# Moving the tiles of a fused decoder layer within the 128-byte grid of on-chip memory

## The chip, the cores and the metric

The kernel runs on one core of one Trainium2 chip. A core has a matrix engine (TensorE, "PE" in the profile; its weight loads are shown apart as "PEld"), three engines for element-wise work (VectorE "DVE", ScalarE "ACT", GpSimd "POOL"), and queues that move data between the chip's main memory and the on-chip memory, which has 128 partitions. The metric is device microseconds of one execution, as the median of the runs.

## The reference

One decoder layer on 256 tokens of 2048 channels, in float32:

```python
hn = rmsnorm(h, attn_norm_w)
u, c_q, c_kv, k_pe = split(hn @ w_in)              # 2048 -> 1024 + 512 + 256 + 64
y_ssm = s5_group(u, ...)                           # 64 groups, diagonal complex scan, GELU, gated unit
y_mla = mla_group(c_q, c_kv, k_pe, ...)            # 8 heads, latent queries, keys, values, causal
h = h + concat(rmsnorm(y_ssm), rmsnorm(y_mla)) @ w_out
a = causal_conv3(rmsnorm(h) @ w_up) + conv_b       # 2048 -> 2 x 5632
gate, val = split(a)
h = h + (silu(gate) * val) @ w_down                # 5632 -> 2048
out = rmsnorm(h, final_norm_w)
```

## The kernel before

Nearly all the work is products with about 180 MB of float32 weights, each read once. The weights come in *chunks* of 128 partitions x 1024 values (512 KB), in a fixed order (`w_in`, the latents' weights, `w_out`, `w_glu`, `w_up`, `w_down`). SP loads a chunk into a tile `raw`. L150 (ACT) rounds it to a part `hi` in a shorter format, L151 (DVE) makes the rest `lo = raw - hi`. Activations are split in the same way. A product is then the sum of three: hi x hi, hi x lo and lo x hi, which `mm3` issues at L165, L166 and L168. So a chunk costs 24 products of 128x128 with 128x256.

`PE.matmul(out, loaded, streamed)` becomes two instructions: a weight load (LDWEIGHTS) that puts the first operand into the array, and a MATMUL that streams the second one past it. In this text *loaded* and *streamed* mean these two operands. Which tile takes which part changes on the way:

- **Input, latents, output projection, gated unit, up-projection** (`mm3`, L165 to L168): `hi` and `lo` of the weights are loaded, 256 tokens of activations are streamed (`xh`/`xl`, `chl`, `ym`, `yhl`, `ys`, `x2h`/`x2l`).
- **Values** (`v_chunk`, L855 to L857): the activations `chl` are loaded, 512 columns of the weights are streamed.
- **Down-projection** (`down`, L1122): the gate's output `hid` (two tiles, `hid0` and `hid1`, the parts hi and lo) is loaded, 512 columns of the weights are streamed. There are four groups of 22 chunks and 12 products per chunk. In the last group the second half of the tokens uses products of 256 columns, and 10 of its 22 chunks have their `hi` and `lo` in tiles `xw` instead (`extra`).

The other parts (state space, attention) run as steps between the chunks up to about 270 us; the string `STEPS` says how many follow each chunk. In the up-projection each of 44 rounds takes four chunks, and its 96 products are followed by the convolution and the gate on ACT, DVE and POOL (`abuf`, `cv`, `hid`; L1069 to L1085).

Tiles are allocated from pools, which are stacked in a partition in the order in which they are opened: `const` (small tables, with the packed parameters `pk` first), `wp` (`hi`, `lo`, `raw`), `mid` (`uT`, `u4`, `yT`), `cpool` (`cA`, `scr`, `chl`, `qpt`), `sp` (the state space's tiles, later `ys`). After `left1.close()` the place from `mid` on is used again by `fp` (`abuf`, `cv`), `hp_` (`hid`) and `wx` (two more `raw` buffers: two of each five chunks from then on use them). `r0` (`xh`, `xl`, `x2h`, `x2l`, `ym`, `yhl`, `hT`, `ho`, `xw`) is stacked from the other end. A tile's place is rounded up to a multiple of 32 bytes. So a tile that grows moves every tile that is stacked after it.

Of the kernel before, what the change touches and what calls it, by code (L numbers as in the profile page):

```python
# [11 lines left out]
F32 = mybir.dt.float32  # L12
# [5 lines left out]
PSUM = bass.MemoryType.PSUM  # L18

P = 128  # L20
# How many steps of the state space follow each chunk of weights until its output is needed: the chunks
# of u, of the latents, of keys, values and queries, the last heads, the attention half of the output.
# [15 lines left out]
# Column layout of the packed per-partition parameters.  # L38
# [16 lines left out]
def layer_kernel(ctx: ExitStack, tc: tile.TileContext, pack, pos, xt, bk, w_in, w_kpe, w_uqn,  # L55
# [17 lines left out]
    # every chunk: 128 partitions x up to 1024 values, split exactly into two float32r parts  # L73
# [53 lines left out]
    def load_after(dst, src):  # L127
        """A load that stays behind the weights asked for so far."""
        with tc.issue_after(state["last"]):
            SP.dma_start(dst, src)  # L130

    def w_prep_to(n):
        while state["prep"] < min(n, len(chunks)):
            i = state["prep"]
            w_dma_to(i + 1)
            raw = raws.pop(i)
            if i == KPE_AT + 1:
                # the rotary key is a float32 product with the input rows as they are: its weights take the norm's
                wt = wp.tile([P, 1024], F32, tag="hi", name="wt")
                V.tensor_tensor(out=wt.rearrange("p (k n) -> p k n", n=64),  # L140
                                in0=raw.rearrange("p (k n) -> p k n", n=64),
                                in1=prm("attn_w").unsqueeze(2).to_broadcast([P, 16, 64]), op=ALU.mult)
                splits[i] = (wt, None)
            else:
                if i >= last_down and (i - last_down) % 6 >= 3:
                    hi, lo = extra[(i - last_down) % 6 - 3]
                else:
                    hi = wp.tile([P, 1024], F32R, tag="hi", name="hi")
                    lo = wp.tile([P, 1024], F32R, tag="lo", name="lo")
                A.copy(hi, raw)  # L150
                V.tensor_tensor(out=lo, in0=raw, in1=hi.bitcast(F32), op=ALU.subtract)  # L151
                splits[i] = (hi, lo)
            state["prep"] += 1
            w_dma_to(i + 1 + (5 if more else 3))
# [7 lines left out]
    def mm3(ps, wh, wl, xh, xl, nk, first, last):  # L162
        """ps += sum over k of w[k].T @ x[k], each operand given as two parts."""
        for k in range(nk):
            PE.matmul(ps, wh(k), xh(k), start=(first and k == 0), stop=False)  # L165
            PE.matmul(ps, wh(k), xl(k), start=False, stop=False)  # L166
        for k in range(nk):
            PE.matmul(ps, wl(k), xh(k), start=False, stop=(last and k == nk - 1))  # L168
# [5 lines left out]
    pk = const.tile([P, NPACK], F32, name="pk")  # L174
# [6 lines left out]
    def quads(dtype, name):  # L181
        """Sixteen row tiles, four to a tile."""
        ts = [r0.tile([P, 4, T], dtype, tag=f"xh{i}", name=f"{name}{i}") for i in range(4)]
        return lambda k: ts[k // 4][:, k % 4, :]
# [10 lines left out]

    cA = cpool.tile([P, 2048], F32, tag="cA", name="cA")
    A.dma_start(pk[:, 0:NA0], pack[:, 0:NA0])
    # the first half of the input rows and of three column tiles arrive two row tiles at a time
# [27 lines left out]
    # a few products of ones bring the array to its full clock before the data is there  # L226
# [19 lines left out]
    def tok_sums(parts, ps=None):  # L246
        """Sums over partitions and parts, token t of the half h in column h of a PSUM tile."""
        ps = wk_bank() if ps is None else ps
        for h in range(2):
            for i, a in enumerate(parts):  # L250
                PE.matmul(ps[:, h:h + 1], a[:, 128 * h:128 * h + 128], ones[:, 0:1], start=(i == 0),
                          stop=(i == len(parts) - 1))
        return ps[:, 0:2]

    def tok_rsqrt(ps, n, eps=None):
        """1 / sqrt(ps / n + eps) by token."""
        r = const.tile([P, 2], F32, tag="rtok", bufs=6, name="rtok")
        A.activation(r, ps, AF.Sqrt, bias=eps_t if eps is None else eps, scale=1.0 / n)
        V.reciprocal(out=r, in_=r)
        return r  # L260

    def tok_rows(r):
        """The values by token as a row, alike in every partition."""
# [6 lines left out]
    def row_scale(dst, parts, n, eps=None):  # L270
        """dst[p, t] = 1 / sqrt(sum over partitions and parts / n + eps), alike in every row."""
# [4 lines left out]
    def split_scaled(hi, lo, src, w):  # L276
        """hi + lo = src * w (one value of w per partition), hi in float32r."""
# [26 lines left out]
    def wrap(dst, src, k):  # L304
        """dst = src less the nearest multiple of 2 pi."""
# [14 lines left out]
    # factors of the complex products, the second set for the imaginary part of the other operand  # L320
# [6 lines left out]
    def ssm_setup():  # L327
# [21 lines left out]
        # columns: powers 0..4 of the state layout, then the key layout, each step with its own power  # L349
# [9 lines left out]
        # phase of a chunk of four steps in turns, and in two parts of which one has few bits  # L359
# [24 lines left out]
        # z = (abar - 1) / lambda  # L384
# [18 lines left out]
        # z times the powers, pair index outermost: [re | -im] and [-im | -re]  # L403
# [23 lines left out]
    # cos and sin of i * phi for the 64 chunks, eight pairs at a time  # L427
# [28 lines left out]
    # matrices of the state space, four pairs of groups at a time  # L456
# [8 lines left out]
    def ssm_in_products(b):  # L465
        """Chunk inputs to states times abar, laid [(step, p32), ...]: the two halves of the complex products."""
# [18 lines left out]
    def ssm_out_mats(b, c):  # L485
        """States (times abar) to outputs: C z abar^l, real (c = 0) and negated imaginary part."""
# [40 lines left out]
    def ssm_k(b):  # L527
        """Lag matrices: values of input b against C z abar^l."""
# [11 lines left out]
    def ssm_m(b):  # L540
        """Within a chunk: lag matrices placed by step, the skip on the diagonal."""
# [70 lines left out]
    def ssm_main():  # L612
        """Three steps per batch, each meant to follow one chunk of weights."""
# [54 lines left out]
    def u_pre(i):  # L668
# [8 lines left out]
        elif i == 8:  # L677
            load_after(pk[:, NA1:], pack[:, NA1:])
# [35 lines left out]
    def kpe_chunk():  # L714
        """The 64 channels of the rotary key, twice: even row tiles on one half of the array's columns, odd on the other."""
# [56 lines left out]
    # The latents stay without their scales by token: that of the queries goes into the softmax, those  # L772
    # of keys and values are applied where these leave PSUM.
# [9 lines left out]
    def c_norm():  # L783
        """rx / sqrt(mean((rx * latent) ** 2) + eps) by token, of the queries and of keys and values."""
# [11 lines left out]
        # of the two halves of the tokens the second comes first, as in the scores  # L796
# [33 lines left out]
    # queries and keys of two heads to a tile; their outputs, scaled and in two parts, take their place  # L830
# [170 lines left out]
    # sigmoid(z) = (1 + tanh(z / 2)) / 2; the group is held doubled until its norm  # L1001
# [47 lines left out]
    abuf = [fp.tile([P, 2, T + 2], F32, name=f"abuf{i}", bufs=1) for i in range(2)]  # L1049
# [38 lines left out]
    # Tokens on the partitions, two halves of them; the channels as (a, row tile, i), where 32 a + i is the  # L1088
    # partition a channel had. One group of weights has the 512 channels of one a.
# [4 lines left out]
    def ho_load():  # L1094
        """The residual to tokens on partitions: blocks of 32 x 32 turned, then moved."""
# [18 lines left out]
    # sums of squares: three groups and the two halves of the last  # L1114
# [19 lines left out]
    def finish(h, m):  # L1134
        """The norm by token: m of the sums ahead of the last."""
# [16 lines left out]
    # in the last group the second half of the tokens stays behind, and has a bank for each half of the channels  # L1152
# [120 lines left out]
```

## Time and profile before

| | |
|---|---|
| median of 3 runs | 1112.39 us (1111.87 to 1112.79) |
| span of the profiled execution, first to last instruction | 1111.5 us |
| instructions, TensorE products among them | 20545, 8264 |
| TensorE busy | 1066.4 us, 96% of the span |
| VectorE, ScalarE, GpSimd busy | 736.2, 611.0, 286.0 us |
| moved by DMA | 195.40 MB, mean 176 GB/s |
| mean granted TensorE clock | 0.991 of full speed |

The profiled execution is told by its span alone; what lies around the span shows only in that the runs' median is 0.9 us longer. A MATMUL row's duration covers the whole way of a product through the array, and the next product starts long before it ends. The *pitch*, from the start of one product to the start of the next, is what a product costs in a row of them. The timeline merges neighbours that are alike into one row with a count, so the pitch is the difference of two rows' starts by the count. The row of stages below (windows) gives each engine's busy time in a stretch with the number of its instructions.

### The profile page before, as it was taken

Reading aid. Unit: us, or ns where it says so; the run is one execution under the profiler, and the core shown is the slowest. Engines: PE = TensorE matmul, PEld = TensorE weight load, DVE = VectorE, ACT = ScalarE, POOL = GpSimd, SP = SyncE. Lnnn points to the kernel's source line nnn. Section 1 sums busy time; section 2 is a strip of 40 time slices with the busy share of each in tenths; the row PEclk is TensorE's granted clock in tenths of the full one; section 3 lists DMA queues with packets and bytes.
Section 4 is the critical chain, followed back from the end, with each engine's and each line's share of the span. In section 5 each row is a group of like instructions: output and inputs, shape, how many; then the busy total and the mean of one; then the engine's idle time right before and its main releaser. Section 6 shows DMA issues by size and latency. Waiting matters only on the chain.

```text
span 1111.5 us, 20545 instructions
## 1 busy us (share of the span) xinstructions
PE 1066.4 (96%) x8264; PEld 1002.9 (90%) x8264; DVE 736.2 (66%) x998; ACT 611.0 (55%) x986; POOL 286.0 (26%) x284
## 2 busy tenths in 40 slices
PE   7979899787999999999999999999999999999997
PEld 7979877786999999999999999999999888888896
DVE  8999898797798665656566565665657545454543
ACT  6567578857765645555555455555554434343433
POOL 7371745773333121211212112121211000000000
PEclk9989999999999999999999999999999999999999
DMA  6635341433555455555555555555555965555652
GB/s 211 227 115 172 134 130 61 171 134 131 173 176 186 172 189 189 174 188 180 182 189 183 180 189 174 188 189 180 182 182 185 258 227 189 189 189 189 210 190 76
DMA packets 56672, 195.40 MB, mean 176 GB/s; under 512 B 6528, under 2 KB 8448, under 8 KB 56576
## 3 DMA queue, kind: packets, MB, share of 16 engines
q1 hardware_dynamic: 54576, 190.93, 50.0%
q10 hardware_dynamic: 2000, 3.16, 1.1%
q8 instruction: 65, 1.06, 0.4%
q14 instruction: 31, 0.25, 0.1%
HBM read 189.86 MB, written 2.10 MB: 173 GB/s over the span
## 4 chain that ended last, share of the span: by engine, by line
PE 78%; DVE 11%; ACT 5%; issue 3%; DMA 3%; POOL 0%; SPq 0%; ACTq 0%; DVEq 0%
PE mm L168 18%; PE mm L166 18%; PE mm L165 18%; PE mm L1122 11%; PE wk L1122 11%; DVE lo L151 3%; ACT yT L610 1%; DMA bkt<-in_bk_dram 1%; DVE epad L477 1%; PE wk L913 1%; DVE hT L992 1%; PE wk L912 1%; ACT u L512 1%; DMA raw<-in_w_in_dram 1%; DVE sh L578 1%
## 5 line engine op out<-in xcount | busy, mean ns | idle before, releaser
L151 DVE TENSOR_TENSOR lo<-raw,hi 128x1024 fp32r<-128x1024 f32 x329 | 411.4, 1252 | 256.0 <-ACT hi L150 253.5
L150 ACT CAST hi<-raw 128x1024 fp32r<-128x1024 f32 x329 | 343.4, 1047 | 305.8 <-PE mm L166 113.2
L166 PE MATMUL mm<-x2l,hi 128*128 128x256 f32 x1408 | 345.6, 283 | 0.0
L165 PE MATMUL mm<-x2h,hi 128*128 128x256 f32 x1408 | 345.6, 283 | 0.0
L165 PEld LDWEIGHTS mm<-x2h,hi 128*128 128x128 f32 x1408 | 270.3, 192 | 0.0
L166 PEld LDWEIGHTS mm<-x2l,hi 128*128 128x128 f32 x1408 | 270.3, 192 | 0.0
L168 PE MATMUL mm<-x2h,lo 128*128 128x256 f32 x1408 | 197.6, 283 | 0.0
L168 PEld LDWEIGHTS mm<-x2h,lo 128*128 128x128 f32 x1408 | 181.6, 192 | 0.0
L1083 POOL TENSOR_TENSOR cv<-cv 128x256 f32<-128x256 f32 x44 | 68.0, 1545 | 389.4 <-ACT cv L1082 375.8
L1122 PE MATMUL wk<-hi,hid 128*128 128x512 f32 (+1 forms) x360 | 88.1, 364 | 0.0
L1122 PE MATMUL mm<-hi,hid 128*128 128x512 f32 x312 | 85.4, 395 | 0.0
L1122 PEld LDWEIGHTS wk<-hi,hid 128*128 128x128 f32 x360 | 63.5, 188 | 13.0
L1069 DVE TENSOR_TENSOR abuf<-mm,r 128x512 f32<-128x512 f32 x43 | 29.7, 691 | 62.2 <-PE mm L168 62.2
L1122 PEld LDWEIGHTS mm<-hi,hid 128*128 128x128 f32 x312 | 57.8, 188 | 13.1
L1075 ACT ACTIVATE cv<-abuf,pk 128x256 f32<-128x256 f32 x88 | 48.3, 595 | 28.5 <-DVE abuf L1069 26.9
L1084 ACT CAST hid<-cv 128x256 fp32r<-128x256 f32 x44 | 17.9, 406 | 75.1 <-POOL cv L1083 71.8
L1122 PE MATMUL wk<-lo,hid 128*128 128x512 f32 (+1 forms) x180 | 50.9, 364 | 0.0
L165 PE MATMUL mm<-xh,hi 128*128 128x256 f32 x184 | 48.0, 294 | 2.5 <-ACT hi L150 2.5
L1122 PE MATMUL mm<-lo,hid 128*128 128x512 f32 x156 | 49.0, 395 | 0.0
L166 PE MATMUL mm<-xl,hi 128*128 128x256 f32 x184 | 47.6, 292 | 0.0
L493 POOL TENSOR_TENSOR m<-bkt,pp 128x256 f32<-128x256 f32 x32 | 30.2, 955 | 61.2 <-DMA bkt<-in_bk_dram 47.2
L610 ACT ACTIVATE yT<-wk 32x64 f32<-32x64 f32 x128 | 35.6, 278 | 7.8 <-PE wk L604 6.3
(330 smaller groups left out, 1641.4 us busy)
## 6 DMA issues: line engine op xcount, KB each, us to landing
raw<-in_w_up_dram SPq DMA_DIRECT2D x176, 512.0 KB, 3.2
raw<-in_w_down_dram SPq DMA_DIRECT2D x88, 512.0 KB, 4.2
raw<-in_w_out_dram SPq DMA_DIRECT2D x32, 512.0 KB, 3.3
raw<-in_w_in_dram SPq DMA_DIRECT2D x25, 512.0 KB, 3.3
bkt<-in_bk_dram SPq DMA_DIRECT2D x8, 512.0 KB, 5.6
raw<-in_w_glu_dram SPq DMA_DIRECT2D x8, 512.0 KB, 3.3
raw<-in_w_uqn_dram SPq DMA_DIRECT2D x4, 512.0 KB, 4.3
hT<-in_xt_dram SPq DMA_DIRECT2D x4, 512.0 KB, 4.9
```

What stands on the lines that cost most here:

```text
L150: A.copy(hi, raw)
L151: V.tensor_tensor(out=lo, in0=raw, in1=hi.bitcast(F32), op=ALU.subtract)
L165: PE.matmul(ps, wh(k), xh(k), start=(first and k == 0), stop=False)
L166: PE.matmul(ps, wh(k), xl(k), start=False, stop=False)
L168: PE.matmul(ps, wl(k), xh(k), start=False, stop=(last and k == nk - 1))
L493: G_.tensor_tensor(out=m, in0=ci[:, s].unsqueeze(2).to_broadcast([P, 4, 4, 16]), in1=pp[:, s, c].rearrange("p (q l) -> p q l", l=4)[:, cb, ...
L610: A.activation(dst[:, j], psy[32 * j:32 * j + 32, q], AF.Gelu_apprx_tanh)
L1069: V.tensor_tensor(out=a[:, :, 2:T + 2], in0=ps, in1=r2.unsqueeze(1).to_broadcast([P, 2, T]), op=ALU.mult)
L1075: A.activation(t, a[:, gv, 2:T + 2], AF.Identity, bias=prm("conv_b", ch_, 1), scale=prm("conv_w", 176 + ch_, 1))
L1083: G_.tensor_tensor(out=cv[0], in0=cv[0], in1=cv[1], op=ALU.mult)
L1084: A.copy(hid[0][:, i, :], cv[0])
L1122: PE.matmul(ps[:, 0:n], hid[x][:, 2 * i + k, ts_], w[wk][:, 512 * k + c0:512 * k + c0 + n], start=(i == 0 and s == 0 and k == 0), stop=(i ...
```

## The change

Three tiles grow by bytes that nothing reads, and so what is stacked after them moves. The engines' instructions, their order, their sizes and their waits are those of before; only places differ, and with them the step from partition to partition of two tiles.

```diff
-    pk = const.tile([P, NPACK], F32, name="pk")
+    pk = const.tile([P, NPACK + 16], F32, name="pk")
...
+    cpool.tile([P, 16], F32, name="gap")
     cA = cpool.tile([P, 2048], F32, tag="cA", name="cA")
...
-            load_after(pk[:, NA1:], pack[:, NA1:])
+            load_after(pk[:, NA1:NPACK], pack[:, NA1:])
...
-    abuf = [fp.tile([P, 2, T + 2], F32, name=f"abuf{i}", bufs=1) for i in range(2)]
+    abuf = [fp.tile([P, 2, T + (12, 2)[i]], F32, name=f"abuf{i}", bufs=1) for i in range(2)]
```

The rest of the diff takes out comments; the line numbers in this text up to the next section are those of the kernel before. `pk` grows by 64 bytes per partition, `gap` takes another 64, `abuf0` grows by 80 (64 after rounding). The places that the two built programs give, in bytes from a partition's start, with the remainder by 128 and by 512:

| tiles | first byte before | mod 128, mod 512 | first byte after | mod 128, mod 512 |
|---|---|---|---|---|
| `hi`, `lo` of `wp` (first `hi`) | 30432 | 96, 224 | 30496 | 32, 288 |
| `raw` of `wp` (first) | 55008 | 96, 224 | 55072 | 32, 288 |
| `raw` of `wx` (first) | 169760 | 32, 288 | 169888 | 32, 416 |
| `uT`, `u4`, `yT` of `mid` (`uT`) | 67296 | 96, 224 | 67360 | 32, 288 |
| `chl` | 91872 | 96, 224 | 92000 | 96, 352 |
| `ys` | 108256 | 96, 224 | 108384 | 96, 352 |
| state space's tiles of `sp` (`epad`) | 108256 | 96, 224 | 108384 | 96, 352 |
| `xh`/`x2l`/`ym`/`qk` of `r0` (first) | 180192 | 96, 480 | 180192 | 96, 480 |
| `xl`/`hT`/`xw` of `r0` | 196576 | 96, 480 | 196576 | 96, 480 |
| `x2h`/`yhl`/`ho` of `r0` | 212960 | 96, 480 | 212960 | 96, 480 |
| `hid0` | 79648 | 32, 288 | 79776 | 32, 416 |
| `hid1` | 124704 | 32, 288 | 124832 | 32, 416 |
| `abuf0`, `abuf1` | 67296, 69376 | 96 and 0 (mod 128) | 67360, 69504 | 32 and 0 (mod 128) |
| `kpe` of `const` | 26912 | 32, 288 | 26976 | 96, 352 |

Slices of these tiles start a multiple of 512 bytes further on (128 columns) or of 1024 (256 columns), so all slices that a product takes have their tile's remainder by 512.

## The prediction

> **What bounds the kernel now.** I read the page's first sections, then one table of the stages, then the timeline of TensorE inside the long stages, and last the chain of waits in the short ones.
>
> ```profile
> PE 1066.4 (96%) x8264; PEld 1002.9 (90%) x8264; DVE 736.2 (66%) x998; ACT 611.0 (55%) x986; POOL 286.0 (26%) x284
> ...
> PEclk9989999999999999999999999999999999999999
> ...
> PE 78%; DVE 11%; ACT 5%; issue 3%; DMA 3%; POOL 0%; SPq 0%; ACTq 0%; DVEq 0%
> ```
>
> TensorE is busy nearly throughout, it is 78% of the chain that ends last, and its clock is granted at 90% or more in nearly every slice. The stages (input, latents and heads, attention half of the output with the state space, gated unit, state-space half of the output, up, down, the last group of down):
>
> ```profile
> core 0: us, PE busy (x) PEld busy (x) DVE busy (x) ACT busy (x) POOL busy (x), PEclk, DMA share, GB/s
> 0.00:116.80 116.80, 103.07 (x800) 97.99 (x801) 104.81 (x164) 78.25 (x131) 62.14 (x73) 0.96 0.52 177
> 116.80:174.00 57.20, 51.89 (x439) 43.62 (x438) 51.75 (x89) 40.47 (x86) 34.31 (x34) 1.00 0.37 123
> 174.00:269.00 95.00, 79.61 (x977) 72.14 (x978) 76.75 (x126) 69.52 (x200) 60.93 (x64) 0.98 0.33 116
> 269.00:303.50 34.50, 31.49 (x244) 30.72 (x243) 26.35 (x36) 26.84 (x55) 8.56 (x10) 0.95 0.58 201
> 303.50:350.40 46.90, 46.90 (x394) 46.90 (x393) 44.10 (x66) 28.69 (x48) 16.61 (x15) 1.00 0.52 179
> 350.40:858.00 507.60, 507.60 (x4233) 507.60 (x4232) 310.95 (x402) 265.96 (x356) 101.98 (x88) 1.00 0.53 183
> 858.00:1043.80 185.80, 185.80 (x799) 149.76 (x799) 92.36 (x87) 77.15 (x84) 1.48 (x2) 1.00 0.64 204
> 1043.80:1103.60 59.80, 59.80 (x394) 54.07 (x392) 27.21 (x29) 21.71 (x27) 0.00 (x0) 1.00 0.42 148
> ```
>
> From 303.5 us on TensorE never idles. The up-projection alone is 507.6 us, with VectorE busy 61% and ScalarE 52%: there a product's pitch is the time. The change can act only through that pitch, so the question is whether the pitch depends on the places of the two operands. The program before already holds products with different places. In the timeline of TensorE, the up-projection (loaded `hi`/`lo` at 96, streamed `x2h`/`x2l` at 96):
>
> ```profile
> 500.09 1.12 PE L168 MATMUL mm<-x2h,lo 128*128 128x256 f32 x8
> 501.05 0.28 PE L165 MATMUL mm<-x2h,hi 128*128 128x256 f32 x1
> ```
>
> Eight products in 0.96 us: a pitch of 120.0 ns, for 256 columns. In the last group of down (loaded `hid` at 32, streamed `xw` or `hi`/`lo` at 96):
>
> ```profile
> 1062.37 1.53 PE L1122 MATMUL wk<-xw,hid 128*128 128x256 f32 x12
> 1063.73 1.56 PE L1122 MATMUL mm<-xw,hid 128*128 128x512 f32 x6
> 1065.13 0.62 PE L1122 MATMUL wk<-hi,hid 128*128 128x256 f32 x4
> 1065.59 0.39 PE L1122 MATMUL wk<-lo,hid 128*128 128x256 f32 x2
> 1065.81 0.62 PE L1122 MATMUL wk<-hi,hid 128*128 128x256 f32 x4
> ```
>
> Twelve products of 256 columns in 1.36 us are 113.3 ns each, and six with `hi` and `lo` in 0.68 us are 113.3 again. Same shape, same type, one weight load per product: 6.67 ns less. It makes no difference whether the streamed tile lies at byte 196576 or 30432; the remainder by 128 is what these rows have in common and the up-projection has not. The weight loads agree:
>
> ```profile
> L165 PEld LDWEIGHTS mm<-x2h,hi 128*128 128x128 f32 x1408 | 270.3, 192 | 0.0
> ...
> L1122 PEld LDWEIGHTS wk<-hi,hid 128*128 128x128 f32 x360 | 63.5, 188 | 13.0
> ```
>
> 192 ns where both operands stand at 96, 188 ns where they stand 64 apart.
>
> For 512 streamed columns it is the other way round. The six products at 1063.73 us above (loaded 32, streamed 96) take 1.40 us, 233.3 ns each. The values stream 512 columns with both operands at 96:
>
> ```profile
> 155.07 0.40 PE L855 MATMUL mm<-hi,chl 128*128 128x512 f32 x1
> ...
> 156.46 0.39 PE L855 MATMUL mm<-hi,chl 128*128 128x512 f32 x1
> ...
> 169.50 0.39 PE L857 MATMUL mm<-lo,chl 128*128 128x512 f32 x1
> ...
> 170.86 0.39 PE L857 MATMUL mm<-lo,chl 128*128 128x512 f32 x1
> ```
>
> The first six, from 155.07 to 156.46 us, have 231.7 ns; the last six, from 169.50 to 170.86 us, 226.7 ns. Twice the pitch of 113.3 is 226.7, so these run free and the down-projection pays 6.67 ns per product, again. Why the sign turns is not shown; the table allows one reading: with 256 columns the loads run without a break (PEld 507.60 of 507.60 us), so each load trails its product, while with 512 they pause (149.76 of 185.80) and each starts along with its product.
>
> **The change part by part.** No instruction is added, removed or reordered on any engine or queue; every term is a count times a pitch.
>
> *Up.* `hi`/`lo` go to 32, `x2h`/`x2l` stay at 96. By 512 that is 288 loaded and 480 streamed, exactly the pair of `hid` and `xw` above. 44 x 4 x 24 = 4224 products x 6.67 ns = **28.2 us**; TensorE has no idle time there, so all of it shows if the chunks keep up. Who waits for whom in 356 to 866 us, then in 866 to 1109 us:
>
> ```profile
> ACT hi L150 <- PE mm L166: 82.6, 47, 1.9
> ...
> ACT hi L150 <- PE wk L1122: 109.7, 63, 3.5
> ...
> ACT xw L150 <- DMA raw<-in_w_down_dram: 5.6, 3, 2.8
> ```
>
> ScalarE waits for TensorE to free a buffer, not TensorE for ScalarE. The stage would take 479.4 us and need 183 x 507.6 / 479.4 = 194 GB/s; down already moves 204.
>
> *Down, 512 columns.* Streamed `hi`/`lo` come to 32, where `hid` stays: equal places, as in the values. The first three groups have 66 x 12 = 792 products x 6.67 ns = 5.3 us gained. In the last group 12 chunks have their parts in `wp`: 72 more such products gain 0.5 us, and 144 products of 256 columns go to equal places and lose 1.0 us. The 10 `xw` chunks keep their places. Together **4.8 us** gained. Bounds: the row of 226.7 ns on one side; on the other, equal places cost 512 columns another 6.67 ns, which is 864 x 6.67 = 5.8 us and the 1.0 us lost. I take the values' row, since it is the only one with 512 columns and equal places, and six products after a change of pattern were still at 231.7.
>
> *The stages before.* All other streamed activations (`xh`, `xl`, `chl`, `ym`, `yhl`, `ys`) end at 96 over weights at 32 and can gain only where products carry the chain. The chain of waits in 116.8 to 174, 174 to 269, 269 to 303.5 and 303.5 to 350.4 us:
>
> ```profile
> by line: PE wk L912 10.1%; PE wk L913 10.0%; DMA bkt<-in_bk_dram 8.9%; PE mm L168 7.1%; DVE lo L151 7.0%; PE mm L166 6.9%; PE mm L165 6.8%; issue 6.1%; DVE gm L481 3.7%; POOL m L493 3.3%; PE mm L855 3.2%; PE mm L856 3.2%; PE mm L857 3.2%; D
> ...
> by line: issue 15.7%; ACT yT L610 12.7%; DVE hT L992 8.0%; DVE lo L151 7.2%; DVE epad L477 6.0%; DVE sh L578 4.5%; ACT mt L552 4.3%; DVE scr L991 3.8%; DVE e L471 3.6%; PE wk L913 2.6%; DVE ta L569 2.5%; DVE tb L570 2.5%; DVE gm L481 2.5%;
> ...
> by line: PE mm L168 30.7%; PE mm L166 23.1%; PE mm L165 20.8%; ACT yT L610 12.9%; ACT hi L150 5.5%; ACT yhl L1009 4.8%; DVE yhl L1010 2.0%; issue 0.8%
> ...
> by line: PE mm L168 33.0%; PE mm L166 33.0%; PE mm L165 32.7%; PE wk L266 0.9%; PE wk L251 0.7%
> ```
>
> Products are 74.6% of 34.5 us in the gated unit: 25.7 us, 214 products, **1.4 us**. In the state-space half of the output they are all of it, 384 products, 2.6 us; but VectorE is busy 44.1 of 46.9 us and would have 44.3 left, so it is late next: I take half, **1.3 us**. In the heads 20.8% of 57.2 us is 99 products, 0.7 us, less 24 value products that lose up to 6.67 ns: **0.5 us**. Between 174 and 269 us and before 116.8 us products hardly carry the chain: **0.2 us**, and at most another 3 us if waits close up.
>
> *Other engines.* Whether a place costs them is seen at L151, which reads `raw` at 96 for three of five chunks and at 32 for two. Five in a row in the up-projection:
>
> ```profile
> 501.86 1.22 DVE L151 TENSOR_TENSOR lo<-raw,hi 128x1024 fp32r<-128x1024 f32 x1
> ...
> 504.57 1.22 DVE L151 TENSOR_TENSOR lo<-raw,hi 128x1024 fp32r<-128x1024 f32 x1
> ...
> 507.81 1.23 DVE L151 TENSOR_TENSOR lo<-raw,hi 128x1024 fp32r<-128x1024 f32 x1 [2.02 <-ACT hi L150]
> ...
> 510.05 1.23 DVE L151 TENSOR_TENSOR lo<-raw,hi 128x1024 fp32r<-128x1024 f32 x1 [1.02 <-ACT hi L150]
> ...
> 513.38 1.22 DVE L151 TENSOR_TENSOR lo<-raw,hi 128x1024 fp32r<-128x1024 f32 x1
> ```
>
> 1.22 or 1.23 us in all: nothing is put down for them.
>
> The sum is 28.2 + 4.8 + 1.4 + 1.3 + 0.5 + 0.2 = 36.4 us. The span of 1111.5 becomes 1075.1; with the 0.9 us by which the median of the runs is longer, **1076.0 us**.
>
> **The rivals.** *A, as above.* Chance 0.68, 1071 to 1080 us.
>
> *B, up gains but down does not.* After the change the operands of down agree by 128 but not by 512 (288 and 416), while those of the values agreed by both. Without the 4.8 us the time is 1080.8; at the far bound (6.8 us lost instead) 1087.6. Chance 0.14.
>
> *C, nothing happens.* The 6.67 ns might come from something else that sets the two stages apart, such as 24 products in a row into one bank of results against 6. Against it: the values, six in a row into one bank, have both 231.7 and 226.7. Time 1112.4, chance 0.05. The Trainium skill has a rule that speaks for this rival ("TensorE: Matmul & The Clock Gate", section "Step-by-step: what each phase is for"): the array reads the streamed operand and the weights by two independent ports, and loading the next weights does not take bandwidth from the running product. By that rule no place could matter and the sum would be zero; the rows of 113.3 and 120.0 ns, alike in all but the tiles, do not fit it.
>
> *D, slower.* One mechanism: equal places cost 6.67 ns at any width, and up's 120.0 ns has another cause. Then down pays 5.8 + 1.0 us and the time is 1119. It decides once up gains less than 6.8 / 4224 = 1.6 ns per product. For it speaks that equal places are what up has now; against it the 226.7 of the values. Chance 0.04.
>
> *E, the chunks come late.* Up's gain turns into waits of L150 for `raw`; with half of it left, 1090 us. Against it the 204 GB/s of down. Chance 0.06.
>
> **How the numbers follow.** The remaining 0.03 lies below 1071, if the early stages close up by more. The range 1071 to 1088 holds A and B, 0.82. A, B, E and the rest are faster by over 0.2% (2.2 us, about what a measurement of this kernel can tell from no change): 0.91. C is within it, 0.05, and D beyond, 0.04.
>
> **What would show it.** Right: rows of eight L168 products 0.91 us apart, weight loads of 188 ns in up, the stage 28 us shorter; six products of 512 columns in 1.36 us; products of 256 columns with `hi` in the last group at 120. Wrong: 120.0 ns in up (C, D), 233 or 240 in down (B), or idle TensorE with L150 waiting for DMA (E).

## The result, and the profile after

| | before | after |
|---|---|---|
| median (range) | 1112.33 us (1111.87 to 1112.79, 4 runs) | 1101.42 us (1100.62 to 1102.56, 4 runs) |
| span of the profiled execution | 1111.5 us | 1098.8 us |
| mean granted TensorE clock | 0.991 | 0.983 |

The time ratio is 0.9896 (0.9882 to 0.9910): about 11 us faster, where 36.4 us had been predicted. The sign is right, the size is not, and the time lies above the range. The two spans in the table differ by 12.7 us, more than the medians, because the profiled execution of after is the fastest of its four. The page of the kernel after, in the lines that answer to those shown of before (busy time by engine, then shares of the chain that ended last):

```profile
PE 1056.1 (96%) x8264; PEld 993.3 (90%) x8264; DVE 736.6 (67%) x998; ACT 611.5 (56%) x986; POOL 285.1 (26%) x284
...
PE 80%; DVE 9%; ACT 5%; DMA 3%; issue 2%; POOL 0%; SPq 0%; ACTq 0%; DVEq 0%
```

The counts are those of before; TensorE is busy for 10.3 us less and VectorE, ScalarE and GpSimd for the same time within 1 us. The windows by stage (input, latents and heads, attention half with the state space, gated unit, state-space half, up, three groups of down, last group):

```profile
core 0: us, PE busy (x) PEld busy (x) DVE busy (x) ACT busy (x) POOL busy (x), PEclk, DMA share, GB/s
0.00:116.60 116.60, 102.67 (x799) 97.47 (x800) 104.66 (x164) 78.57 (x131) 62.55 (x74) 0.93 0.53 177
116.60:174.20 57.60, 53.40 (x441) 44.92 (x439) 52.81 (x89) 40.77 (x88) 33.16 (x34) 0.97 0.37 123
174.20:269.50 95.30, 81.10 (x976) 73.97 (x976) 77.01 (x126) 69.36 (x200) 60.83 (x64) 0.93 0.35 115
269.50:301.10 31.60, 28.55 (x243) 27.73 (x242) 25.91 (x36) 26.60 (x55) 8.53 (x10) 1.00 0.65 218
301.10:347.20 46.10, 46.10 (x395) 46.10 (x394) 44.19 (x66) 28.78 (x48) 16.64 (x15) 1.00 0.55 183
347.20:845.00 497.80, 497.80 (x4233) 497.80 (x4232) 310.85 (x402) 266.09 (x356) 101.96 (x88) 1.00 0.56 187
845.00:1030.40 185.40, 185.39 (x800) 150.04 (x799) 92.99 (x88) 77.55 (x84) 1.48 (x2) 1.00 0.65 207
1030.40:1091.20 60.80, 60.80 (x393) 55.21 (x391) 26.23 (x29) 21.69 (x28) 0.00 (x0) 1.00 0.42 141
```

Up is 9.8 us shorter instead of 28.2. Down as a whole is 0.6 us longer instead of 4.8 shorter (0.4 gained, 1.0 lost). The gated unit is 2.9 us shorter, the state-space half 0.8. TensorE still has no idle time in up, so what is missing there is pitch and no wait. These are windows of one execution each: the shorter gated unit stands at a granted clock of 1.00 beside 0.95 before, which is taken up below. The timeline of TensorE at the start of up says more:

```profile
346.25 1.10 PE L168 MATMUL mm<-ys,lo 128*128 128x256 f32 x8
...
349.02 1.07 PE L168 MATMUL mm<-x2h,lo 128*128 128x256 f32 x8
...
351.74 1.07 PE L168 MATMUL mm<-x2h,lo 128*128 128x256 f32 x8
...
354.46 1.07 PE L168 MATMUL mm<-x2h,lo 128*128 128x256 f32 x8
...
357.18 1.07 PE L168 MATMUL mm<-x2h,lo 128*128 128x256 f32 x8
358.09 0.50 PE L254 MATMUL wk<-ones,hacc 128*128 128x1 f32 x4
...
360.41 1.11 PE L168 MATMUL mm<-x2h,lo 128*128 128x256 f32 x8
```

The starts of 349.02, 351.74, 354.46 and 357.18 us are 2.72 us apart, and 24 products lie in each step: 113.3 ns, the predicted pitch. Then four float32 products of one column pass (`wk<-ones,hacc`, the row sums of a norm). From there to the end of up, but for a gap in the second round where more products of the norm pass, the starts are 117 to 119 ns apart and the mean pitch is 117.8 ns, with the same tiles at the same places. One weight load in three then takes 192 ns and the others 187 or 188, so that the mean of up falls between the two values that the prediction named:

```profile
L165 PEld LDWEIGHTS mm<-x2h,hi 128*128 128x128 f32 x1408 | 266.5, 189 | 0.0
```

The timeline in the first groups of down, and in the last group (each kernel's rows have its own line numbers; L1125 here is L1122 of before):

```profile
899.79 1.10 PE L1125 MATMUL wk<-hi,hid 128*128 128x512 f32 x4
900.73 0.62 PE L1125 MATMUL wk<-lo,hid 128*128 128x512 f32 x2
901.19 1.09 PE L1125 MATMUL mm<-hi,hid 128*128 128x512 f32 x4
...
1043.46 1.57 PE L1125 MATMUL wk<-xw,hid 128*128 128x256 f32 x12
1044.87 1.09 PE L1125 MATMUL mm<-hi,hid 128*128 128x512 f32 x4
...
1054.67 0.64 PE L1125 MATMUL wk<-hi,hid 128*128 128x256 f32 x4
1055.14 0.41 PE L1125 MATMUL wk<-lo,hid 128*128 128x256 f32 x2
1055.38 0.65 PE L1125 MATMUL wk<-hi,hid 128*128 128x256 f32 x4
```

Six products of 512 columns take 1.40 us as before (233.3 ns; over all those with `hi` and `lo` the mean is 232.4 ns after and 233.2 before), though their operands are now at equal places by 128. In the last group the 256-column products with `hi` and `lo` take 118.3 ns (0.71 us by six), as the sign of the prediction had it. But those with `xw` take 117.5 ns (1.41 us by twelve) instead of 113.3, and those were to keep their pitch. The rows of 512 columns and those with `xw` speak against a remainder by 128.

### The profile page after: what moved, and what is told of

It is laid out like the page before. It is cut to its first block, busy times and chain, and to the rows that moved or that the text cites. A ratio compares the mean times of both kernels' runs of the same rounds, so it can differ in the third digit from the quotient of the medians.

```text
span 1098.8 us, 20545 instructions
## 1 busy us (share of the span) xinstructions
PE 1056.1 (96%) x8264; PEld 993.3 (90%) x8264; DVE 736.6 (67%) x998; ACT 611.5 (56%) x986; POOL 285.1 (26%) x284
## 4 chain that ended last, share of the span: by engine, by line
PE 80%; DVE 9%; ACT 5%; DMA 3%; issue 2%; POOL 0%; SPq 0%; ACTq 0%; DVEq 0%
PE mm L168 18%; PE mm L166 18%; PE mm L165 18%; PE wk L1125 11%; PE mm L1125 11%; DVE lo L151 2%; DMA raw<-in_w_in_dram 2%; ACT yT L613 2%; ACT hi L150 1%; DVE epad L480 1%; PE wk L916 1%; DVE hT L995 1%; PE wk L915 1%; ACT u L515 1%; DVE sh L581 1%
## 5 line engine op out<-in xcount | busy, mean ns | idle before, releaser
L151 DVE TENSOR_TENSOR lo<-raw,hi 128x1024 fp32r<-128x1024 f32 x329 | 411.0, 1251 | 249.3 <-ACT hi L150 249.0
L166 PE MATMUL mm<-x2l,hi 128*128 128x256 f32 x1408 | 339.6, 281 | 0.0
L165 PE MATMUL mm<-x2h,hi 128*128 128x256 f32 x1408 | 339.4, 281 | 0.0
L165 PEld LDWEIGHTS mm<-x2h,hi 128*128 128x128 f32 x1408 | 266.5, 189 | 0.0
L166 PEld LDWEIGHTS mm<-x2l,hi 128*128 128x128 f32 x1408 | 265.7, 189 | 0.0
L168 PE MATMUL mm<-x2h,lo 128*128 128x256 f32 x1408 | 194.4, 281 | 0.0
L168 PEld LDWEIGHTS mm<-x2h,lo 128*128 128x128 f32 x1408 | 178.6, 189 | 0.0
L1125 PE MATMUL wk<-hi,hid 128*128 128x512 f32 (+1 forms) x360 | 88.3, 364 | 0.0
L1125 PE MATMUL mm<-hi,hid 128*128 128x512 f32 x312 | 85.3, 395 | 0.0
L1125 PEld LDWEIGHTS wk<-hi,hid 128*128 128x128 f32 x360 | 63.9, 188 | 12.6
L1125 PEld LDWEIGHTS mm<-hi,hid 128*128 128x128 f32 x312 | 57.9, 188 | 13.1 <-ACT hi L150 0.4
L1125 PE MATMUL wk<-lo,hid 128*128 128x512 f32 (+1 forms) x180 | 51.1, 365 | 0.0
L1125 PE MATMUL mm<-lo,hid 128*128 128x512 f32 x156 | 48.9, 394 | 0.0
```

The source lines that it names most:

```text
L1125: PE.matmul(ps[:, 0:n], hid[x][:, 2 * i + k, ts_], w[wk][:, 512 * k + c0:512 * k + c0 + n], start=(i == 0 and s == 0 and k == 0), stop=(i ...
```

## The experiments

Two questions: which remainder counts, and what the two pitches in up are. Places are given as distance, the streamed tile's place less the loaded one's. Experiments 1 to 4 ran first, beside one another.

**Theory after the result.** The pitch follows from the distance by a larger unit than 128 and, at the distance of up, from a state that a row of equal products keeps. **Rivals:** up is slowed by something else in the layer, such as the chunks that come in, or the clock; or each pair of tiles has one pitch and the first round is an exception.

**1. Products of other widths between the rounds of up (after).** Ahead of each of rounds 5 to 44 stands one more product of 8 to 256 columns, into a bank of results that nothing reads.

```diff
+            if i > 3 and (gv, hf) == (0, 0):
+                kick = wk_bank()
+                PE.matmul(kick[:, 0:KICKS[i - 4]], col(wh, 0), x2h[:, 0, 0:KICKS[i - 4]], start=True, stop=True)
```

> The changed kernel, with one extra product of n columns (n = 8 to 256 in steps of 8, then 20 to 132 in steps of 16) ahead of each of the last 40 rounds of the up-projection; nothing reads its result. The places stay those of the change. Theory 'state': a row of products keeps the pitch it has fallen into (113.3 or 117.8 ns) until a product of another width shifts the loads against the streams. Then rounds differ: after some widths 113.3 ns, after others 117.8 ns, the same for all 96 products of a round; if half of the rounds turn, the time falls by about 20 x 96 x 4.4 ns = 8 us less the price of the extra products (about 40 x 0.1 us). Theory 'place': the pitch follows from the places alone (those of up, 288 and 480 by 512, give 117.8 ns once the first round is over); then all 40 rounds stay at 117.8 ns and the time grows by the extra products, 2 to 6 us.

Measured, in one run: 1097.83 us (before beside it 1113.85). 16 of the 40 rounds ran at 113.3 ns and 24 at 117.8, none between. The timeline of TensorE in this run shows one such turn, at a product of 72 columns:

```profile
482.00 1.11 PE L169 MATMUL mm<-x2h,lo 128*128 128x256 f32 x8
482.94 0.20 PE L1066 MATMUL wk<-x2h,hi 128*128 128x72 f32 x1
...
483.99 0.28 PE L166 MATMUL mm<-x2h,hi 128*128 128x256 f32 x1
...
484.89 0.28 PE L169 MATMUL mm<-x2h,lo 128*128 128x256 f32 x1
```

Eight products before it take 0.94 us, 117.5 ns each; eight products a microsecond later 0.90 us, 112.5 ns by these two decimals. So two pitches exist at one place, a single product of another width switches between them, and the new one lasts at least to the next such product. Chunks that come late, or a clock, would not do that; the granted clock is 1.00 through up.

**2. The same products in the kernel before.**

> The kernel before, with the same extra products in the same 40 rounds. Theory 'state' with place as the gate: equal places (both 96 by 128) have no fast state, all rounds stay at 120.0 ns and the time grows by the extra products, 2 to 6 us. Theory 'state alone': places do not matter, the change only shifted the state by chance; then some rounds of this kernel too fall to 113.3 or 117.8 ns.

Measured, in one run: 1114.52 us, and all 40 rounds at 119.9 to 120.1 ns. At the places of before none of these 40 products led to a second pitch.

**3. Pairs of places, 256 columns.** The layer's work is left out. Rows of 20 products, from 64 pairs of places (32 + 64i loaded and streamed, within 512) and a few others, each row begun in four ways: directly (`d`), after a product of 64 columns (`h`), after one of 128 (`q`), after two float32 products of one column (`c`).

```diff
+    for a, b in PAIRS:
+        for what, first in (("d", kick_none), ("h", kick_64), ("q", kick_128), ("c", kick_col)):
+            first(a, b)
+            p = ps.tile([P, 512], F32, tag="p", name=f"{what}{a}on{b}x")
+            for j in range(ROW):
+                PE.matmul(p[:, 0:N], ld(a, j), st(b, j), start=(j == 0), stop=(j == ROW - 1))
```

> The layer's work is left out. The kernel only issues rows of 20 products of 256 columns from one loaded and one streamed tile, for 76 pairs of places (all 64 pairs of 32 + 64 i by 512, and 12 pairs with a place that is a multiple of 64), each pair four times: directly after the pair before, after a product of 64 columns, of 128 columns, and after two float32 products of one column. Theory 'state': one pair shows more than one pitch, by what went before it, and pairs that agree by 128 show 120.0 ns always. Theory 'place': one pair has one pitch after all four, and it is 117.8 or 113.3 ns by a bit above 128 (loaded 288 with streamed 480 against loaded 32 with streamed 96).

**4. The same with 512 columns**, rows of 10 products.

> The same with rows of 10 products of 512 columns; the layer's work is left out. In the two kernels equal places showed 226.7 ns (values, equal by 512) and 232.7 ns (down after the change, equal by 128 but 128 apart by 512), places 64 apart 233.3 ns. Theory 'place': equal by 512 gives 226.7 ns after all four beginnings, 128 apart 232 to 233 ns. Theory 'state': both give 226.7 ns after some beginnings and 231 to 236 ns after others.

Measured, as mean pitch in ns at the end of the rows (the last 10 with 256 columns, the last 6 with 512), by the distance's remainder by 256. The pitch is taken from the starts of single products in the trace. These are the 64 pairs; the very first row of each run (213.3 and 348.3 ns), begun before the trace's clock record starts at full speed, is left out:

| distance mod 256 | 256 columns | 512 columns |
|---|---|---|
| 0 | 119.7 to 120.0 | 226.7 to 231.5 |
| 64 | 117.7 to 117.9 | 228.7 to 230.7 |
| 128 | 118.6 to 120.0 | 230.8 to 233.5 |
| 192 | 113.3 in 36 rows, 117.8 in 28 | 233.2 to 234.2 |

Four rows of the timeline of experiment 3 (the name gives the beginning and the places, loaded "on" streamed; a row's length also holds its first products, which are uneven, so it is not 20 times the pitch of the table):

```profile
376.88 2.54 PE L67 MATMUL d288on288x<-x,w 128*128 128x256 f32 x20
...
387.09 2.52 PE L67 MATMUL d288on352x<-x,w 128*128 128x256 f32 x20
...
407.38 2.45 PE L67 MATMUL d288on480x<-x,w 128*128 128x256 f32 x20
...
409.70 2.60 PE L67 MATMUL h288on480x<-x,w 128*128 128x256 f32 x20
```

The last two are the pair of up after the change (288 loaded, 480 streamed), fast when begun directly and slow after 64 columns. In all 16 pairs of distance 192 the row after 64 columns has the other of the two pitches than the row begun directly, so one pair has two pitches, by what passed ahead. Pairs whose distances differ by 256 agree (within 512), and distances 128 apart do not: this is the period.

Among the 12 other pairs, one of distance 64 (0 loaded, 64 streamed) also had 113.4 ns after one beginning and 117.7 to 117.9 after the other three, so two pitches are not the property of distance 192 alone. With 512 columns distance 192 is the slowest. Distance 0 has three levels there: 226.7 ns in 4 rows of 63, 228.3 to 228.8 in 32 and 231.0 to 231.5 in 27. So the theory 'place' of experiment 4 fails too, and 226.7 ns is the best state of its distance, not its only pitch.

Here lies the Trainium skill's rule that the prediction weighed ("TensorE: Matmul & The Clock Gate", section "Step-by-step: what each phase is for"): by it, loading the next weights takes no read bandwidth from the running product. In this grid, one shape and one load per product take 113.3 to 120.0 ns by the distance of their places, so for these float32r products (the shorter format of `hi` and `lo`) the two operands are not independent in time, and what the prediction drew from the rule, that no place could matter, does not hold. By what path the two meet is not shown.

**5. One product of 128 columns in the third round (after).** The cheapest attempt to set the pitch of 113.3 ns once.

```diff
+            if i == 2 and (gv, hf) == (0, 0):
+                kick = wk_bank()
+                PE.matmul(kick[:, 0:128], col(wh, 0), x2h[:, 0, 0:128], start=True, stop=True)
```

> The changed kernel with one extra product of 128 columns at the start of the third of the 44 rounds of up, and nothing else. In the run with 40 extra products a width of 128 turned a round from 117.8 to 113.3 ns, and the rounds kept what they had. Theory 'state': rounds 3 to 44 run at 113.3 ns, 42 x 96 x 4.44 ns = 17.9 us less: 1083.5 us. Theory 'place alone' or 'each round falls back': at most 0.4 us, 1101 us.

Measured: 1102.85 us, ratio to before 0.9911 (0.9891 to 0.9932); up stayed at 117.8 ns. A miss: in experiment 1 a product of 128 columns had turned 117.8 ns into 113.3, here it did not. The width alone does not decide; whether it is the place in a pattern, or something else not seen, stays open.

**6. `hid` moved to equal places by 256 (after).**

```diff
-    abuf = [fp.tile([P, 2, T + (12, 2)[i]], F32, name=f"abuf{i}", bufs=1) for i in range(2)]
+    abuf = [fp.tile([P, 2, T + (28, 2)[i]], F32, name=f"abuf{i}", bufs=1) for i in range(2)]
```

> The changed kernel with abuf0 64 bytes longer per row pair again (T + 28 instead of T + 12), so that hid moves by 128 bytes: its remainder by 128 stays 32, by 256 it goes from 160 to 32, that of hi and lo. Theory 'the difference counts by 256': products of 512 columns go from 232.7 ns to 226.7, or to 228.7 to 231.3 if the other state is met; 864 of them, 5.2 us less, 1096 us (1.2 to 3.5 us less in the other state). Theory 'by 128': nothing changes, 1101.4 us.

Measured: 1097.36 us, ratio 0.9859 (0.9840 to 0.9877). The timeline in down, and the window of its first three groups:

```profile
900.15 1.07 PE L1125 MATMUL wk<-hi,hid 128*128 128x512 f32 x4
901.06 0.61 PE L1125 MATMUL wk<-lo,hid 128*128 128x512 f32 x2
901.51 1.07 PE L1125 MATMUL mm<-hi,hid 128*128 128x512 f32 x4
```
```profile
848.30:1030.30 182.00, 180.81 (x799) 149.41 (x799) 91.48 (x86) 77.13 (x83) 1.48 (x2) 1.00 0.67 208
```

Six products take 1.36 us, 226.7 ns, and the stage 182.0 us instead of 185.4. The gain that the prediction gave to down is there, but at distance 0 by 256.

**7. The kernel before with 128 bytes added to `pk`.** All remainders by 128 stay those of before; the weights' `hi` and `lo` move by 128 against the activations.

```diff
-    pk = const.tile([P, NPACK], F32, name="pk")
+    pk = const.tile([P, NPACK + 32], F32, name="pk")
...
-            load_after(pk[:, NA1:], pack[:, NA1:])
+            load_after(pk[:, NA1:NPACK], pack[:, NA1:])
```

> The kernel before with pk 128 bytes longer and nothing else: every tile of the stack from the left moves by 128, so all remainders by 128 are those of before (weights 96, activations 96, hid 32). By 256 the streamed x2h and x2l come to stand 128 from the loaded hi and lo. Theory 'by 256': up falls from 120.0 to 118.2 to 118.8 ns, 5 to 7.6 us less, 1105 to 1107 us, if the state that keeps 120.0 is not met; the half of the output for the state space stays at 120.0 and down at 233.3. Theory 'by 128': 1112.4 us and 120.0 ns everywhere.

Measured: 1108.06 us, ratio 0.9960 (0.9944 to 0.9976). The windows of the state-space half, of up and of down:

```profile
302.80:349.70 46.90, 46.90 (x394) 46.90 (x393) 44.24 (x66) 28.72 (x48) 16.80 (x15) 1.00 0.53 179
349.80:851.80 502.00, 502.00 (x4234) 502.00 (x4233) 310.89 (x402) 265.97 (x356) 101.68 (x88) 1.00 0.55 185
851.90:1037.50 185.60, 185.60 (x798) 149.57 (x797) 91.62 (x87) 77.22 (x84) 1.48 (x2) 1.00 0.65 205
```

Up goes from 507.6 to 502.0 us (118.7 ns, the grid's value for distance 128); the other two, whose loaded and streamed tiles moved together, stay. By a rule of 128 nothing could have changed. With the grid, where distances 256 apart agree, the unit is 256.

**8. Experiments 5 and 6 together, with `gap` of 48 columns** (which brings `ys` to distance 192).

> All together: the changed kernel with the one extra product of 128 columns in the third round, hid moved by 128 as above, and gap 128 bytes longer, which puts chl and ys 192 from the weights by 256 as xh and x2h are. Sum of the parts: 17.9 + 5.2 us, and up to 384 x 4.4 ns = 1.7 us in the half of the output for the state space if VectorE lets it: 1077 us. If one of the states is not met: 1082 us without the fast state in down, 1095 us without that in up.

Measured: 1097.04 us, ratio 0.9854 (0.9835 to 0.9872). The state-space half ran at 113.8 ns and down at 226.9, but up stayed at 117.8, so the time is near the 1095 us named for that case.

**9. The same width again and again** (places of experiment 8): rounds 3 to 12 begin with 192 columns, the next ten with 200, then 208, then 184; the last three groups of ten begin with 120 instead.

```diff
+            if i > 1 and (gv, hf) == (0, 0):
+                kick = wk_bank()
+                n = 120 if i in (12, 22, 32) else (192, 200, 208, 184)[(i - 2) // 10 if i < 42 else 3]
+                PE.matmul(kick[:, 0:n], col(wh, 0), x2h[:, 0, 0:n], start=True, stop=True)
```

> The kernel of the run before (all parts together), with an extra product ahead of every round from the third on: 192 columns in rounds 3 to 12, 200 in 13 to 22, 208 in 23 to 32, 184 after that, but 120 columns at the start of the last three groups, a width that threw a fast round back to 117.8 ns. With 40 different widths 192, 200 and 208 left a fast round fast, and 128, which turned a slow one there, did nothing as a single product. Theory 'state, with the place in its pattern': what an extra product does depends on where in the repeating pattern of three pitches it comes, so one width turns a slow round only sometimes; a width that keeps fast rounds fast then holds the state once it is met, and a group has slow rounds first and fast ones after. Theory 'width decides': all rounds of a group are alike from its second round on.

Measured, in one run: 1087.86 us. After 192 columns all ten rounds were fast, the first turned from slow. 120 columns turned fast to slow each of three times. After 200 all nine were fast, the first again turned from slow; after 208 two slow, then seven fast; 184 switched to and fro in every round. The 184 and the 208 speak against 'width decides': one width led to both pitches.

**10. Distances in steps of 8 bytes, 256 columns** (experiment 3's rows, 23 products long, loaded at 256 or 288).

> The layer's work is left out. Rows of 23 products of 256 columns, loaded at 256 or 288, streamed 0 to 248 bytes further in steps of 8, each pair with the four beginnings of the coarse grid. If the pitch follows the distance in steps of a whole 64 bytes, there are four levels (120.0; 117.8; about 118.5; 113.3 or 117.8) with borders between them; if it is finer, some distance near 192 may have 113.3 ns after all four beginnings, which would make the fast state sure.

Measured, in ns: 120.0 at 0, 117 to 118 at 32, 117.8 at 64, 120 at 96, 113.3 to 114.7 at 112 after all four beginnings, 119 to 120 at 128, 117 to 119 at 160, 113.3 or 117.8 at 192, 118 to 119 at 224; odd multiples of 8 from 118.0 to 123.4, mostly over 119.5. So there are no four levels with borders between them: the pitch changes with steps of 8 bytes, and the table's classes hold for places on the grid of 64 only. Distance 112 was not tried in the layer.

**11. 192 columns at the start of rounds 3, 4 and 5 (after).**

```diff
+            if i in (2, 3, 4) and (gv, hf) == (0, 0):
+                kick = wk_bank()
+                PE.matmul(kick[:, 0:192], col(wh, 0), x2h[:, 0, 0:192], start=True, stop=True)
```

> The changed kernel with an extra product of 192 columns at the start of rounds 3, 4 and 5 of up, all places as in the change. In the run with repeated widths 192 turned a slow round and left fast ones fast, ten times of ten. Theory 'state': from round 3 on up runs at 113.3 ns, 42 x 96 x 4.44 = 17.9 us less, 0.3 us for the extra products: 1083.8 us against the 1101.4 of the change. This is what the prediction had for up, less the two rounds ahead. If the state is not held in every execution, the runs spread between 1084 and 1101.

Measured: 1085.18 us (1083.5 to 1087.0), ratio 0.9743 (0.9730 to 0.9757). Up runs at 113.3 ns from the third round to its end, through all 40 rounds of 96 products after the last extra one; from its first product to its last it takes 480.3 us instead of 497.8. The window from 345 to 830 us, which holds up, the us ahead of it and the first few us of down:

```profile
345.00:830.00 485.00, 485.00 (x4263) 484.39 (x4262) 315.20 (x409) 268.82 (x357) 102.50 (x89) 1.00 0.59 193
```

TensorE is busy for all of it at 193 GB/s: the chunks keep up. Three products whose results nothing reads bring 16 to 17 us more than the change alone (16.2 as 1101.42 less 1085.18; the two were timed on different occasions, and by the ratios to before it is 17.0). Whether the first of the three would have been enough was not tried.

**12. The same products with the places of experiment 8.**

> All places as in the run of all parts together (hid at the weights' place by 256, chl and ys 192 away), and the three extra products of 192 columns. The sum: 1097.0 of that run less 17.6 us: 1079.4 us, which is the time predicted for the change alone, by 3 us. If up falls back, 1097.

Measured: 1078.57 us (1078.13 to 1082.2), ratio 0.9691 (0.9676 to 0.9706): the best version. Up 113.4 ns, state-space half 113.6, down 226.9. The windows of up and of the first groups of down:

```profile
345.00:825.00 480.00, 480.00 (x4234) 480.00 (x4233) 310.60 (x402) 267.30 (x355) 103.42 (x89) 1.00 0.60 193
830.00:1005.00 175.00, 174.28 (x769) 143.96 (x769) 85.97 (x79) 73.25 (x79) 1.47 (x2) 1.00 0.68 211
```

TensorE's 4234 products in 480.00 us are 113.4 ns each; 769 of down in 174.28 us are 226.6.

## Why the prediction was wrong in size

- **That the time is TensorE's pitch and that places set it: right.** The grid shows it with nothing of the layer around; rivals C (nothing happens), D (slower) and E (late chunks) fall: up gained, by more per product than D's bound, and TensorE did not idle.
- **Up, 28.2 us: the term was mis-sized; it measured 9.8.** The step that failed is "exactly the pair of `hid` and `xw` above", from which one pitch was taken. It is that pair, and it has two pitches. The row read in the last group of down showed only one of them. The prediction's own rows held a warning: the values, one pair of places, showed 231.7 and 226.7 ns, and the question of two pitches was not put to up. Up ran at 113.3 ns for its first round and at 117.8 after. Experiment 11 sets the state and gets the rest: up as a whole is then 17.5 us shorter, of the 18.4 that were missing. Why the twelve `xw` products of before were fast stays open. That they follow products of 512 columns is not enough: in experiment 6 `xw` over `hid` is at distance 192 again and follows them too, yet twelve take 1.42 us, 118 ns each:

```profile
1046.13 1.58 PE L1125 MATMUL wk<-xw,hid 128*128 128x256 f32 x12
1047.55 1.07 PE L1125 MATMUL mm<-hi,hid 128*128 128x512 f32 x4
```

- **Down, 4.8 us: failed; it lost 0.6.** The step was "equal places, as in the values", with equality by 128. Rival B had named the doubt: 288 and 416 are 128 apart and not equal. Experiment 6 shows the 226.7 ns at distance 0 by 256. The loss of the 144 products with `hi` came about (113.8 to 118.7 ns), but not by equal places. "The 10 `xw` chunks keep their places" was false: `hid` moved by 128, so their distance went from 192 to 64 and their pitch from 113.7 to 117.8 ns.
- **The inference behind both.** "The remainder by 128 is what these rows have in common" was one of two readings, as the rows at hand agreed by 256 too. `x2h` over `hi` before was 480 less 224, which is 256: distance 0. Read that way, the prediction's rows fall into the grid's classes for distance 0 (up, the values) and 192 (down). The weight loads agreed for 256 columns only: in down they take 188 ns at 233.3 ns per product, and 187 or 188 in experiment 6 at 226.7.
- **Stages before, 3.4 us: near in sum (3.2), and that is luck.** Up began at 350.4 us in the trace of before and at 347.8 in that of experiment 2, with the same places; with the places of the change up to there it began at 347.2 (after), 346.7, 351.1, 350.4 and 346.3 us (experiments 1, 5, 6, 11). So 3.2 us is within what programs that are alike up to there differ by from trace to trace. The gated unit's 2.9 us instead of 1.4 are mostly the clock: the record of before has 3.4 us at half clock there, from 278.8 us on, that of after has none. The same stage with the places of before at full clock (experiment 2), and with the places of the change with such a stretch (experiment 6):

```profile
268.40:300.80 32.40, 29.97 (x243) 29.22 (x242) 25.68 (x35) 25.91 (x54) 8.71 (x10) 1.00 0.64 214
```
```profile
270.20:304.30 34.10, 31.07 (x244) 30.26 (x243) 26.28 (x36) 26.78 (x55) 8.58 (x10) 0.95 0.59 202
```

Against 31.6 us after and 34.5 before, the places are worth 0.8 us at full clock and 0.4 us with the stretch. The pitch at distance 192 is not fixed there either: 114.0 ns in the trace of after, 118.2 and 117.7 in those of experiments 5 and 6, whose programs are the same up to there; in experiment 5 the stage takes 32.5 us at full clock, no gain at all. The state-space half gained 0.8 us instead of 1.3, in every trace (47.0 us with distance 0, 46.1 with 64, at 117.8 ns; experiments 8 and 12 bring it to 113.6 to 113.8 ns). Input, heads and attention half gained nothing together (+0.5 us instead of -0.7), although the input's pitch fell from 120 to between 114 and 116 ns; the prediction's chain gives products little part there, and the granted clock was lower in all three (0.93, 0.97 and 0.93 after, 0.96, 1.00 and 0.98 before), which one execution does not separate. The values lost, as was allowed for, and went from 229 to 233 ns.

- **Other engines, nothing: right.** L151, in the costliest groups, takes 1251 ns with its tiles moved, and 1252 before:

```profile
L151 DVE TENSOR_TENSOR lo<-raw,hi 128x1024 fp32r<-128x1024 f32 x329 | 411.0, 1251 | 249.3 <-ACT hi L150 249.0
```

Open: what lies behind 256 bytes, why the order of distances turns with 512 columns, and what the state is. The prediction's reading (loads that trail their products with 256 columns and start with them with 512) is not borne out: in the trace of before, each weight load starts 2 or 3 ns after a product has started, in up (400 to 800 us) as in down (870 to 1030 us). That the float32 products threw up out of its 113.3 ns is seen in the trace of after, where the turn follows them; it was not tried by taking them away.

## What to carry to other kernels

Where products follow one another without a gap, read the pitch from the timeline and compare it over rows with one shape; a difference without a wait can be a matter of the operands' places, here of their distance by 256 bytes. Before a period is taken from a few rows, list all rows with all candidate periods, and test the smallest one with one shift that, by it, changes nothing. A pitch read in one place may be one of two states: look for rows of the same pair elsewhere, and for what passed just ahead of them. Before the gain of a short stage is put down to a change, compare its granted clock, and other traces with the same places.

## What was not expected of the hardware

- Same instruction, same tiles, two steady pitches: 113.3 and 117.8 ns. One product of 192 columns at the start of the third round turned the slow one to the fast in three runs of three (experiments 9, 11, 12), and after the last of three such products it lasted through 40 rounds of 96.
- The best place depends on the width: on the grid of 64 bytes, distance 192 has the best pitch with 256 columns (113.3 ns, in one of its two states) and the worst with 512 (233.2 to 234.2); distance 0 has 120.0 ns with 256 and the best with 512 (226.7, in one of its three).
- The whole of it is worth 3.1% here: 1078.57 us with all places and the state set, and no work taken away.
